# A trunk layer with three gated branches: every engine and the DMA queue run in the planner's order

## The chip, the cores and the metric

The kernel runs on one core of a Trainium2 chip. A core has a matrix engine (TensorE, PE in the profile), three engines for elementwise work (VectorE or DVE, ScalarE or ACT, GpSimd or POOL) and SyncE (SP), whose queue here issues every DMA. The engines run side by side, each through its own list of instructions from first to last, and wait for one another by semaphores. The metric is the device time of one execution in microseconds (us), taken as the median of several runs.

## The reference, cut to what is computed

One layer over 2048 tokens of width 1024. Every product with a weight is done in fp32 accuracy.

```python
h = rms_norm(x, norm_g)
z = h @ w_in
(aq, ak, av, af, az, bq, bk, bv, ba, bb, bz, mq, mz, gates) = _split_cols(z, IN_SIZES)
o_a = forgetting_attention(aq, ak, av, af + b_fg)      # 8 heads of 64
y_a = o_a * silu(az)
qkv = silu(causal_dwconv(concat([bq, bk, bv]), conv_w))
o_b = gated_delta_rule(gq, gk, gv, g_log, beta)        # 4 heads of 128
y_b = rms_norm(o_b, gdn_norm_g) * silu(bz)
mk, mv = split(rms_norm(mem, mem_norm_g) @ w_mem_kv)   # 256 memory rows
y_m = softmax(mq @ mk.T * scale) @ mv * silu(mz)
proj = einsum('bsnc,ncd->bsnd', stack([y_a, y_b, y_m]), w_branch)
merged = sum(sigmoid(gates + b_merge) * proj, axis=2)
return rms_norm(x + merged @ w_out, final_norm_g)
```

## The kernel before

The work is laid out over tokens in four groups of 512 and over features in blocks of 128. Each operand is split into a rounded part and a remainder (`hh` and `hl` for the activations, `wh` and `wl` for the weights), and `mm3k` multiplies them in three matmuls (L401, L402, L403). These "dense" jobs, made by `dense()`, are the bulk of PE's work; one weight block of 128 columns serves up to four groups (96 matmuls). Its path: a load `wr_in` by SP, a cast to `wh_in` on ACT (L381), the remainder `wl_in` on POOL (L385). Each result leaves PSUM through ACT and DVE (`evh` and `evl` for split results, `evt`, `evs`, `evg` for the others) and is stored to DRAM by SP (`dqh`, `dql`, `dgt` and so on).

The rest is written as generators that come one after another in `part_side`: norm (`part_norm`, which calls `rms_transposed`), logits (`part_logits`), memory attention, the chunks of the delta rule (`part_gdn_a`), their inverses (`part_gdn_inv`), the recurrence (`part_gdn_b` with `chain` and `tail`) and forgetting attention (`part_fox`). The last stages, branch projections (`pbr`, `pba`) and output projection (`pout`), belong to the dense part.

In the norm a tile of 128 tokens is loaded (`xt`), squared and summed on ACT (L342) or DVE (L335, `jkv`), its scale worked out on DVE (L347 and L293 to L298), multiplied in place (L352, `xt`), transposed on PE in two halves (L360, `ptx`), cast on ACT to `hh` (L362) and subtracted on DVE to `hl` (L363). Group 0 goes tile by tile, the other three in batches of four tiles.

In the logits, `pslg` on PE is followed by a chain of ACT and DVE steps that ends in a scan on DVE (L572, `loc`), a transpose on PE (`ptlg`) and a store `dG`. The inverse is a long row of small DVE steps (L901, L903) in the tiles `bk` and `tmp`, stored as `dinv`; the values `pd_v` leave through `evx` to the stores `dv` meanwhile. Forgetting attention clears its tiles `QA` and `KA` on DVE (L1115 to L1120), takes maxima of the scores `psm` (L1185, L1188), transposes them (`ptm`) and then makes the scores `pst` again for the exponent.

What sets the order: the class `Plan` (L25) holds a model of the time. Each generator yields the time from which its next PE step can run and what that step costs; `run` takes the first part that is ready at the modelled PE time, dense work being last in the list, and so emits the program. The costs are estimates (`act`, `dve`, `pool`, `dma`: an operation of n columns on DVE counts 0.15 + 0.00105 n us, a DMA 0.45 us of SP and at least 3 us to land), and `Ring` and `Banks` keep the modelled times at which PSUM comes free. `load_w`, `Feed` and `Stores` place weight loads and stores at modelled times in the same way. After that the framework has a scheduler of its own, which lays out each engine's list anew: by data dependences and its own estimates it may move an instruction past another of the same engine, DMAs on SP's queue included. The planner's order is thus only a suggestion to it.

Of the kernel before, what the change touches and what calls it, by code (L numbers as in the profile page):

```python
# [19 lines left out]
P = 128  # L20
EPS = 1e-6
INF = float("inf")
# [184 lines left out]
def four(ps):  # L207
    return ps.rearrange("p (a b) -> p a b", a=4)
# [3 lines left out]
def tile_trunk(ctx, tc, x, mem, norm_g, w_in, w_v, w_lg, b_fg, b_mg, conv_w, a_log, dt_b,  # L212
               gdn_g, mem_g, w_kv, w_br, w_out, final_g, out):
    nc = tc.nc
# [7 lines left out]
    pl = Plan()  # L222
# [20 lines left out]
    def move(dst, src, kb=0.0, after=0.0):  # L243
        nc.sync.dma_start(dst, src)  # L244
        return pl.dma(kb, after)
# [19 lines left out]
    dzb = [dram.tile([P, 4, 512], F32, name=f"dzb{g}") for g in range(NG)]  # L265
# [649 lines left out]
    def part_gdn_b():  # L915
# [7 lines left out]
        st = {"S": St0, "lev": 0, "chain": 0, "out": 0}  # L923

        def tmp(nm, tag, n):
            return gb.tile([P, 4, P], F32, tag=tag, name=nm, bufs=n)
# [63 lines left out]
        def chain():  # L990
            yield pl.pe + 2.0, 0.0
            for c in range(NCH):
                g, cc = divmod(c, 4)
# [4 lines left out]
                move(KV, dkv[c], 512)  # L998
                Aq = tmp("Aq", "Aq", 1)
                td = move(Aq, dau[c][:, :, 1, :], 256)  # L1000
                zb = tmp("zb", "zb", 1)
                move(zb, dzb[g][:, :, cc * P:(cc + 1) * P], 256)
                St = st["S"]
                yield later(td, lambda: inv[c][1] - 1.5 if c in inv else INF, rc.when), 0.88
                E, te = inv[c]
                pZ, kb = rc.take("pZ")
# [11 lines left out]
                pY, kb = rc.take("pY")  # L1018
# [8 lines left out]
                pS, kb = rc.take("pS")  # L1027
# [8 lines left out]
                pO, kb = rg.take("pO")  # L1036
                pO = four(pO)
# [2 lines left out]
                    nc.tensor.matmul(pO[:, h], Aq[:, h], Y[:, h], start=False, stop=True)  # L1040
                st["S"] = Sn
                st["chain"] = c + 1
                pl.add(tail(c, pO, kb, zb))

        def tail(c, pO, kb, zb):
            g, cc = divmod(c, 4)
            so = gb.tile([P, 4], F32, tag="so", name="so")
            jk = gb.tile([P, P], F32, tag="jk2", name="jk2")
            for h in range(4):
# [12 lines left out]
            pR, kb = rc.take("pR")  # L1062
# [15 lines left out]
            st["out"] = c + 1  # L1078

        pl.add(chain())  # L1080
        pl.add(levels())
        yield (lambda: 0.0 if st["out"] == NCH else INF), 0.0
# [668 lines left out]
    pl.run(dense())  # L1751


def _layout(i):
    import numpy as np
    c = np.ascontiguousarray
# [45 lines left out]
```

## Time and profile before

| | us |
|---|---|
| runs, median of 3 | 2633.79 (2629.45 to 2636.64) |
| profiled execution, own time | 2629.7 |
| its span | 2627.6 |
| PE busy | 2545.9 |
| DVE busy | 1338.9 |
| ACT busy | 1105.2 |
| POOL busy | 1013.1 |
| mean granted TensorE clock | 0.99 |

The stages in the span, by what PE runs: norm and first projections to 83 us, logits to 165, memory attention among dense jobs to 590, the delta rule's chunks among dense jobs to 1008, values to 1097, gates and recurrence to 1540, forgetting attention among gates to 2024, attention among branch projections to 2330, and the last branch with the output projection to the end. Times in the profile are us from the start of the span. In a row of the timeline stand the start, the duration, the engine, line and operation, and in square brackets how long the engine was idle before it and what ended that. In a row of windows stand the length, then for PE, PEld, DVE, ACT and POOL the busy time (and count of instructions), then the granted clock, the share of the DMA engines and GB/s. The records of matmuls overlap: one of 128 x 512 is 0.39 us long, while the next starts 0.23 us after it.

### The profile page before, as it was taken

The numbers are of one execution on the slowest core, as the hardware profiler recorded it, in microseconds if no ns is written. First come the engines' busy times: TensorE is split into PE (matmuls) and PEld (weight loads), VectorE is DVE, ScalarE is ACT, GpSimd is POOL, SyncE is SP. The second block draws the span as 40 slices with busy tenths as digits, with TensorE's granted clock in tenths as the row PEclk, the third lists the DMA queues.
The fourth block names the chain that finished last, engine by engine and source line by source line (L and its number), as shares of the span: only waits on it lengthen the run. The fifth ranks groups of instructions, "written<-read, shape, count | busy, mean of one in ns | idle before, by whom it ended". The sixth has DMA issues, their size and how long they took to land. (4 is left out here: it accounts for less than half of the span.)

```text
span 2627.6 us, 36711 instructions
## 1 busy us (share of the span) xinstructions
PE 2545.9 (97%) x12648; PEld 2112.2 (80%) x12648; DVE 1338.9 (51%) x2753; ACT 1105.2 (42%) x2287; POOL 1013.1 (39%) x818
## 2 busy tenths in 40 slices
PE   7998999999999999899999999999999999989998
PEld 6787888788888888688888888888887787877887
DVE  7452565656533337702222266666666677635433
ACT  5432234443475532134444446565556445323211
POOL 0101111221144334222232247777776768752110
PEclk9999999999999999999999999999999999999999
DMA  6223222222465564445555454344334768786432
GB/s 205 70 81 109 85 85 92 91 91 86 128 229 201 203 212 149 124 154 166 163 162 171 150 164 134 108 121 120 111 100 117 243 207 251 244 293 213 135 120 75
DMA packets 306050, 391.52 MB, mean 149 GB/s; under 512 B 62524, under 2 KB 185532, under 8 KB 305864
## 3 DMA queue, kind: packets, MB, share of 16 engines
q1 hardware_dynamic: 305864, 389.18, 46.5%
q8 instruction: 100, 1.64, 0.3%
q14 instruction: 86, 0.70, 0.1%
HBM read 238.78 MB, written 150.29 MB: 148 GB/s over the span
## 5 line engine op out<-in xcount | busy, mean ns | idle before, releaser
L401 PE MATMUL pd_in<-hh,wh_in 128*128 128x512 f32 x1856 | 746.6, 402 | 15.2 <-ACT evx L418 12.0
L403 PE MATMUL pd_in<-hh,wl_in 128*128 128x512 f32 x1856 | 728.2, 392 | 0.9
L402 PE MATMUL pd_in<-hl,wh_in 128*128 128x512 f32 x1856 | 726.0, 391 | 0.0
L385 POOL TENSOR_TENSOR wl_in<-wr_in,wh_in 128x1024 fp32r<-128x1024 f32 x84 | 202.5, 2411 | 626.0 <-ACT wh_in L381 597.8
L401 PEld LDWEIGHTS pd_in<-hh,wh_in 128*128 128x128 f32 x1856 | 350.1, 189 | 83.2 <-ACT evx L418 12.4
L403 PEld LDWEIGHTS pd_in<-hh,wl_in 128*128 128x128 f32 x1856 | 348.9, 188 | 78.6 <-POOL wl_in L385 4.0
L402 PEld LDWEIGHTS pd_in<-hl,wh_in 128*128 128x128 f32 x1856 | 350.3, 189 | 64.7
L1301 POOL TENSOR_TENSOR acc<-acc,ph 128x512 f32<-128x512 f32 (+3 forms) x288 | 318.9, 1107 | 55.7 <-ACT ph L1321 41.3
L1321 ACT ACTIVATE ph<-pst 128x512 fp32r<-128x512 f32 (+1 forms) x320 | 170.8, 534 | 159.7 <-PE pst L1315 81.2
L1278 DVE TENSOR_TENSOR plo<-pst,ph 128x512 fp32r<-128x512 f32 (+1 forms) x320 | 192.1, 607 | 83.3 <-ACT pst L1323 80.3
L1323 ACT ACTIVATE pst<-pst 128x512 f32<-128x512 f32 (+1 forms) x320 | 170.6, 533 | 0.0
L1573 POOL TENSOR_TENSOR gt<-gt,pp 128x512 f32<-128x512 f32 x64 | 86.7, 1358 | 191.6 <-DVE gt L1569 157.5
L381 ACT CAST wh_in<-wr_in 128x1024 fp32r<-128x1024 f32 x84 | 88.1, 1049 | 133.7 <-PE pd_in L402 119.2
L1188 DVE TENSOR_REDUCE nmx<-psm 128x1 f32<-128x512 f32 x192 | 128.5, 686 | 26.6 <-PE psm L1181 25.4
L1340 PE MATMUL po<-ph,Vs 128*128 128x512 f32 (+1 forms) x320 | 117.6, 368 | 1.1 <-ACT ph L1321 1.0
L474 DVE SCALAR_TENSOR_TENSOR evv<-xb,cw,evv 128x512 f32<-128x512 f32 x144 | 116.6, 810 | 3.7
L1314 PE MATMUL pst<-QA,KA 128*128 128x512 f32 (+1 forms) x320 | 116.2, 363 | 0.6 <-DVE QA L1196 0.6
L1315 PE MATMUL pst<-QB,KB 128*128 128x512 f32 (+1 forms) x320 | 116.6, 366 | 0.0
L1341 PE MATMUL pq<-plo,Vs 128*128 128x512 f32 (+1 forms) x320 | 116.1, 366 | 0.0
L1181 PE MATMUL psm<-KA,QA 68*128 68x512 f32 (+2 forms) x320 | 110.1, 375 | 4.6 <-DVE nmx L1188 3.0
L1541 PE MATMUL pbr<-yh,wbh 128*128 128x512 f32 x256 | 103.2, 404 | 9.3 <-DVE gt L1569 6.1
L1731 PE MATMUL pout<-woh,mh 128*128 128x512 f32 x256 | 100.1, 393 | 5.5 <-ACT woh L1643 5.5
(343 smaller groups left out, 4752.6 us busy)
## 6 DMA issues: line engine op xcount, KB each, us to landing
wr_in<-in_w_in SPq DMA_DIRECT2D x84, 512.0 KB
dgt<-evg SPq DMA_DIRECT2D x96, 256.0 KB
gt<-dgt SPq DMA_DIRECT2D x96, 256.0 KB
dpt<-gt SPq DMA_DIRECT2D x64, 256.0 KB
pp<-dpt SPq DMA_DIRECT2D x64, 256.0 KB
dgq<-evv SPq DMA_DIRECT2D x48, 256.0 KB
kqv<-dgq SPq DMA_DIRECT2D x16, 768.0 KB
xt<-in_x SPq DMA_DIRECT2D x16, 512.0 KB
```

Source lines behind the costliest of these rows:

```text
L385: nc.gpsimd.tensor_sub(lo, raw, hi.bitcast(F32))
L401: nc.tensor.matmul(ps, wh[:, k, :], xh[:, k, :], start=(k == 0), stop=False)
L402: nc.tensor.matmul(ps, wh[:, k, :], xl[:, k, :], start=False, stop=False)
L403: nc.tensor.matmul(ps, wl[:, k, :], xh[:, k, :], start=False, stop=(k == kt - 1))
L474: nc.vector.scalar_tensor_tensor(t, xb[:, j:j + 512], cw[:, wi, j:j + 1], t, ALU.mult, ALU.add)
L1188: nc.vector.tensor_reduce(mx, ps[:, 0:w], AX.X, ALU.max)
L1278: nc.vector.tensor_sub(plo[:, 0:w], ps[:, 0:w], ph[:, 0:w].bitcast(F32))
L1301: nc.gpsimd.tensor_add(acc[:, c0:512], acc[:, c0:512], ph[:, 0:w].bitcast(F32))
L1315: nc.tensor.matmul(ps[:, 0:w], KB[kt][:, ks], QBn[:, c0:512], start=False, stop=True)
L1321: nc.scalar.activation(ph[:, 0:w], ps[:, 0:w], AF.Exp, scale=0.125)
L1323: nc.scalar.activation(ps[:, 0:w], ps[:, 0:w], AF.Exp, scale=0.125)
L1340: nc.tensor.matmul(po[:, c0:512], V[:, 0:128], ph[:, 0:w], start=(t0 == 0), stop=(t0 == NT - 1))
```

## The change

At the end of the program every instruction of an engine is tied to the one emitted before it on the same engine, by an edge that orders the two for the scheduler and makes no wait on the chip. All five engines, SP with its DMAs among them, thereby get their lists in the order in which `Plan.run` emitted the program; instructions whose class name has "Pool" in it are left out of the chain. Further, the load of `zb` in the recurrence moves from `chain` to `tail`, where it is emitted once the previous chunk's output is out. What is computed stays the same. Line numbers above 1002 shift a little (L1315 before is L1316 now), those ahead of it not at all.

```diff
--- before.py
+++ after.py
@@ -998,8 +998,6 @@
                 move(KV, dkv[c], 512)
                 Aq = tmp("Aq", "Aq", 1)
                 td = move(Aq, dau[c][:, :, 1, :], 256)
-                zb = tmp("zb", "zb", 1)
-                move(zb, dzb[g][:, :, cc * P:(cc + 1) * P], 256)
                 St = st["S"]
                 yield later(td, lambda: inv[c][1] - 1.5 if c in inv else INF, rc.when), 0.88
                 E, te = inv[c]
@@ -1040,10 +1038,13 @@
                     nc.tensor.matmul(pO[:, h], Aq[:, h], Y[:, h], start=False, stop=True)
                 st["S"] = Sn
                 st["chain"] = c + 1
-                pl.add(tail(c, pO, kb, zb))
-
-        def tail(c, pO, kb, zb):
+                pl.add(tail(c, pO, kb))
+
+        def tail(c, pO, kb):
             g, cc = divmod(c, 4)
+            yield (lambda: 0.0 if st["out"] == c else INF), 0.0
+            zb = tmp("zb", "zb", 1)
+            move(zb, dzb[g][:, :, cc * P:(cc + 1) * P], 256)
             so = gb.tile([P, 4], F32, tag="so", name="so")
             jk = gb.tile([P, P], F32, tag="jk2", name="jk2")
             for h in range(4):
@@ -1751,6 +1752,15 @@
     pl.run(dense())
 
 
+    last = {}
+    for i in list(nc.cur_bb.bb.instructions):
+        if isinstance(i, mybir.Instruction) and "Pool" not in type(i).__name__:
+            if i.engine in last:
+                tc.add_manual_dep(i, last[i.engine].name, mybir.DependencyInfo(
+                    mybir.DependencyClass.NoSync, mybir.DependencyReason.DATA), reason="order")
+            last[i.engine] = i
+
+
 def _layout(i):
     import numpy as np
     c = np.ascontiguousarray
```

What this does to the lists is shown at three places. The first is DVE at the start of the program, in the norm of the first two tiles (`bmg` is the bias of the merge gates, scaled by a half once it is loaded). Before:

```order
L465 MEMSET xb 128x3
L347 TENSOR_SCALAR ss<-ss 128x1
L293 RECIPROCAL p0r<-p0s 128x1
L335 SCALAR_TENSOR_TENSOR jkv,ss<-xt 128x1024
L295 TENSOR_TENSOR p0t<-p0r 128x1
L347 TENSOR_SCALAR ss<-ss 128x1
L296 TENSOR_TENSOR p0t<-p0t,ss 128x1
L297 TENSOR_SCALAR p0t<-p0t 128x1
L293 RECIPROCAL p0r<-p0s 128x1
L298 TENSOR_TENSOR rs<-p0r,p0t 128x1
L295 TENSOR_TENSOR p0t<-p0r 128x1
L352 SCALAR_TENSOR_TENSOR xt<-xt,rs,g_bc 128x1024
```

After:

```order
L250 TENSOR_SCALAR bmg<-bmg 128x24
L347 TENSOR_SCALAR ss<-ss 128x1
L293 RECIPROCAL p0r<-p0s 128x1
L295 TENSOR_TENSOR p0t<-p0r 128x1
L296 TENSOR_TENSOR p0t<-p0t,ss 128x1
L297 TENSOR_SCALAR p0t<-p0t 128x1
L298 TENSOR_TENSOR rs<-p0r,p0t 128x1
L352 SCALAR_TENSOR_TENSOR xt<-xt,rs,g_bc 128x1024
L363 TENSOR_TENSOR hl_273<-ptx,hh_269 128x4x128 x2
L335 SCALAR_TENSOR_TENSOR jkv,ss<-xt 128x1024
L347 TENSOR_SCALAR ss<-ss 128x1
L293 RECIPROCAL p0r<-p0s 128x1
```

The scaling of `bmg` stood in row 22 before, behind four `hl` subtractions, and is now ahead of all the norm. The square of tile 1 (`jkv`) was early, now it follows tile 0's two `hl`. In the three later groups of the norm the lists differ in the same manner: four `xt` and then eight `hl` before, `xt` and two `hl` four times now.

The second is SP's queue around the logits (`lgraw`, `lgb` and `lgc` are their weights and constants, `dG` is the store of their scan, `wr_in` the weight of a dense job, `dqh` and `dql` stores of the first projection). Before:

```order
L244 DMA lgraw<-in_w_lg 128x128
L244 DMA lgb<-in_b_fg 8x1
L244 DMA lgb<-in_dt_b 4x1
L244 DMA lgc<-in_a_log 4x1
L244 DMA wr_in_0_1284<-in_w_in 128x1024
L244 DMA dqh_82<-evh 128x512
L244 DMA dql_86<-evl 128x512
L244 DMA wr_in_0_1455<-in_w_in 128x1024
L244 DMA dqh_82<-evh 128x512
L244 DMA dql_86<-evl 128x512
L244 DMA dzm_107<-evt 128x512
L244 DMA dG_140<-loc 4x512
```

After:

```order
L244 DMA lgraw<-in_w_lg 128x128
L244 DMA lgb<-in_b_fg 8x1
L244 DMA lgb<-in_dt_b 4x1
L244 DMA lgc<-in_a_log 4x1
L244 DMA dqh_82<-evh 128x512
L244 DMA dql_86<-evl 128x512
L244 DMA dG_140<-loc 4x512
L244 DMA wr_in_0_1052<-in_w_in 128x1024
L244 DMA dqh_82<-evh 128x512
L244 DMA dql_86<-evl 128x512
L244 DMA dG_141<-loc 4x512
L244 DMA wr_in_0_1113<-in_w_in 128x1024
```

The weights `wr_in_0_1052` and `wr_in_0_1113` stood in rows 10 and 12 before, among the loads of `xt`; now each is behind a store of `dG`.

The third is SP's queue at the end of the values (`dv` are their stores, `dinv` those of the inverse, `dgt` those of the gates). Before:

```order
L244 DMA dv_95<-evx 128x4x128 x8
L244 DMA dinv_194<-bk 128x1024
L244 DMA dinv_194<-tmp 128x1024
L244 DMA bk<-dblk_193 128x1024
L244 DMA dv_96<-evx 128x4x128 x8
L244 DMA dv_97<-evx 128x4x128 x6
L244 DMA dinv_195<-bk 128x1024
L244 DMA dinv_195<-tmp 128x1024
L244 DMA dv_97<-evx 128x4x128 x2
L244 DMA dv_98<-evx 128x4x128 x6
L244 DMA U<-dau_160 128x4x128
```

After:

```order
L244 DMA dv_97<-evx 128x4x128 x8
L244 DMA dv_98<-evx 128x4x128 x6
L244 DMA wr_in_0_9066<-in_w_in 128x1024
L244 DMA dv_98<-evx 128x4x128 x2
L244 DMA dgt_115<-evg 128x512
L244 DMA wr_in_0_9135<-in_w_in 128x1024
L244 DMA dgt_116<-evg 128x512
L244 DMA dgt_115<-evg 128x512
L244 DMA wr_in_0_9204<-in_w_in 128x1024
L244 DMA dgt_116<-evg 128x512
L244 DMA dinv_195<-bk 128x1024
L244 DMA dinv_195<-tmp 128x1024
```

`dinv_195` stood between the stores of `dv_97`; now it is behind all of `dv_98`, four gate stores and three weight loads. At the start of forgetting attention PE's list moves too: before, 27 dense matmuls stood between the fourth `psm` and the first `pst`, and now `ptm`, two `psm` and then `pst` follow it with no dense matmul between. In the last stage 192 `pba` matmuls stand in one block ahead of the first `pout`, where six `pout` came after the first 72 before.

## The prediction

> **What bounds the kernel now.** I read the page's busy shares first, then the windows of 66 us, then PE's waits.
>
> ```profile
> PE 2545.9 (97%) x12648; PEld 2112.2 (80%) x12648; DVE 1338.9 (51%) x2753; ACT 1105.2 (42%) x2287; POOL 1013.1 (39%) x818
> ...
> 0.00:66.00 66.00, 49.50 (x281) 41.36 (x282) 47.55 (x94) 35.87 (x68) 6.45 (x11) 0.97 0.60 204
> 66.00:132.00 66.00, 61.19 (x282) 47.58 (x281) 31.36 (x58) 32.89 (x43) 7.17 (x3) 0.97 0.21 69
> ...
> 1056.00:1122.00 66.00, 53.97 (x224) 43.23 (x223) 44.83 (x63) 14.46 (x33) 20.54 (x26) 0.90 0.45 129
> 1520.00:1586.00 66.00, 65.99 (x301) 53.20 (x300) 43.76 (x108) 28.61 (x55) 31.66 (x35) 1.00 0.50 154
> 1980.00:2046.00 66.00, 60.65 (x259) 47.20 (x258) 41.31 (x91) 36.69 (x77) 46.64 (x42) 0.95 0.52 154
> 2310.00:2376.00 66.00, 54.67 (x310) 47.57 (x308) 24.75 (x29) 16.80 (x24) 38.88 (x27) 0.92 0.79 270
> 2376.00:2442.00 66.00, 62.24 (x354) 54.63 (x353) 31.87 (x66) 18.04 (x37) 13.93 (x9) 0.97 0.56 186
> ```
>
> PE (TensorE) is the bound: busy 2545.9 of 2627.6 us, so only 81.7 us of the span are idle on it. In a stage like 1520 to 1586 it is full (65.99 of 66). It is not full in six windows: the head (16.5 us missing, then 4.8), 1056 to 1122 (12.0), 1980 to 2046 (5.4) and 2310 to 2442 (11.3 and 3.8). The matmuls stay the same, so the change can act in one way only: by making PE wait less there, or more somewhere. PE's waits say for what:
>
> ```profile
> PE pd_in L401 <- ACT evx L418: 12.0, 1, 12.0
> PE ptx L360 <- DVE p0t L296: 9.3, 1, 9.3
> ...
> PE pbr L1541 <- DVE gt L1569: 6.1, 2, 5.0
> PE pout L1731 <- ACT woh L1643: 5.5, 2, 3.1
> ...
> PE ptlg L579 <- DVE loc L572: 3.8, 1, 3.8
> ```
>
> PE's own order hardly moves (after the head it differs by some tens of matmuls). What moves is the order on DVE, ACT, POOL and in SP's queue that feeds PE. So I go through the places where a row that PE waits for stands behind another row than before.
>
> **The first tiles.** The scaling of `bmg` (L250) is now DVE's second row, ahead of the norm of tile 0.
>
> ```profile
> 4.71 0.50 SPq L244 DMA_DIRECT2D bmg<-in_b_mg  x1
> ...
> 5.34 0.15 DVE L347 TENSOR_SCALAR ss<-ss 128x1 f32<-128x1 f32 x1 [4.37 <-ACT jk L342]
> 5.84 1.21 DVE L335 SCALAR_TENSOR_TENSOR jkv<-xt 128x1024 f32<-128x1024 f32 x1
> ...
> 15.93 1.15 DVE L250 TENSOR_SCALAR bmg<-bmg 128x24 f32<-128x24 f32 x1
> ...
> 15.46 0.39 PE L402 MATMUL pdf<-hl,wh_in 128*128 128x256 f32 x1 [1.83 <-DVE hl L363]
> ...
> 25.55 0.38 PE L402 MATMUL pdf<-hl,wh_in 128*128 128x256 f32 x1 [0.22 <-DVE hl L363]
> ...
> DMA packets 974, 3.60 MB, mean 307 GB/s; under 512 B 96, under 2 KB 96, under 8 KB 974
> ...
> DMA packets 491, 0.23 MB, mean 334 GB/s; under 512 B 443, under 2 KB 443, under 8 KB 491
> ```
>
> `bmg` comes in rows of 96 bytes. The last two lines are the DMA views of 0 to 11.7 us (96 such small packets) and of 11.7 to 12.4 (443): behind 3.6 MB the small loads land at about 12.3. Before, L250 stood at 15.93 and held nobody; now tile 0's L347 starts at about 13 in place of 5.34. From there I count: norm chain 1.2, `xt` 1.3, to the first `hl` 2.6, second `hl` 0.6, so tile 0 is done near 18.7. Tile 1's square (1.21 us, L335), done before in the shadow at 5.84, now follows: 1.2 + 1.7 + 1.3 + 2.3 gives 25.5, where the first L402 stood at 15.46. Tiles 2 and 3 follow one after another, some 6.5 us each, so the second half starts near 39 in place of 25.55. **+14 us.** Bounds: +8, if half of the chain overlaps, to +18.
>
> **The other three groups of the norm.** DVE ran all four `xt` (partly beside the previous matmuls), then eight `hl`. Now it runs `xt`, two `hl`, `xt`, two `hl`.
>
> ```profile
> 45.15 3.68 DVE L352 SCALAR_TENSOR_TENSOR xt<-xt,rs,g_bc 128x1024 f32<-128x1024 f32 x3
> ...
> 52.40 1.88 DVE L363 TENSOR_TENSOR hl<-ptx,hh 128x512 fp32r<-128x512 f32 x3
> ...
> 50.97 1.47 PE L360 MATMUL ptx<-ident,xt 128*128 128x128 f32 x12
> 53.13 1.85 PE L360 MATMUL ptx<-ident,xt 128*128 128x128 f32 x12 [0.69 <-DVE hl L363]
> 55.19 1.25 PE L360 MATMUL ptx<-ident,xt 128*128 128x128 f32 x8 [0.21 <-DVE hl L363]
> ...
> 51.65 1.57 ACT L362 CAST hh<-ptx 128x512 fp32r<-128x512 f32 x3
> ```
>
> Before, a group's transposes took 50.97 to 56.5, 5.5 us between dense blocks. Now each tile is a closed circle: `xt` 1.23 (3.68 / 3), to the first half's `hh` 0.1 + 0.68, `hh` to `hl` 0.65 (51.65 + 0.59 is the first end, `hl` follows), two `hl` 1.29: 3.96 us. Group 1 has all four circles behind the last `evl`, 17.6 against 8.3: +9.3. In groups 2 and 3 the first `xt` still stands ahead of the last `evl`: 13.9 against 5.5, +8.4 each. **+26 us.** Bounds +12, if a circle cost only DVE's own 2.5 us, to +30. The memory rows at 196 go through the same helper, two tiles: **+2.**
>
> **The first logits.** The load of `wr_in_0_1052`, issued early before, now stands in SP's queue behind the store of `dG_140`, which waits for the scan L572.
>
> ```profile
> 86.77 0.40 PE L549 MATMUL pslg<-hh,wlh 128*128 128x512 f32 x1
> ...
> 100.49 1.22 DVE L572 TENSOR_TENSOR_SCAN loc<-rmask,l 64x512 f32<-64x512 f32 x1
> ...
> 1008.13 0.33 SPq L244 DMA_DIRECT2D wr_in<-in_w_in  x1
> ...
> 1011.75 1.05 ACT L381 CAST wh_in<-wr_in 128x1024 fp32r<-128x1024 f32 x1 [2.36 <-DMA wr_in<-in_w_in]
> ...
> L385 POOL TENSOR_TENSOR wl_in<-wr_in,wh_in x5: 2383/2390/3046, 10.1 to 115.8; 128x1024 fp32r<-128x1024 f32 x5
> ```
>
> From the end of the logits' matmuls (87.2) to the end of the scan (101.7) are 14.5 us; I take 12.5, since the weight's cast and an eviction leave the chain. Then 0.6 of issue, 4 to 5 us of landing (3.6 at 1008), cast 1.05, POOL 2.4. PE has some 6 us of work in these 21. **+16 us** (bounds +8 to +18). In exchange the wait of 3.8 us for `loc` at 117.5 goes, with its slow spell: **-6.**
>
> **Slow clock.** A stall of 2.6 us is followed by half clock:
>
> ```profile
> 2328.00:2331.00 3.00, 0.36 (x2) 0.00 (x0) 0.00 (x0) 0.00 (x0) 1.16 (x1) 1.00 0.77 225
> 2331.00:2338.00 7.00, 4.64 (x11) 3.69 (x12) 2.92 (x4) 1.85 (x3) 3.39 (x3) 0.52 0.84 292
> ...
> 1106.00:1119.00 13.00, 3.82 (x9) 3.05 (x10) 0.21 (x1) 4.72 (x11) 6.37 (x9) 0.50 0.91 265
> ```
>
> The granted clock is 0.52 for the 7 us after it, with 4.64 us of work: some 2.3 us lost. The longer head has about four sparse stretches more, each ended by dense work at half clock, at 1.7: **+7** (0 to 9). The Trainium skill, page "TensorE: Matmul & The Clock Gate", section "HAM oscillation — how this bites in real kernels", puts the limit at idle gaps over about 3.4 us. By that rule gaps of under 3 us inside the circles would cost no clock and this term would be near 0, the time 7 us lower. The row at 2328, a wait under 3 us, disagrees, so the row stands.
>
> **Values and inverse.** The 12.0 us wait for L418 at 1103: SP's store of `dinv_195`, behind DVE's inverse until 1105, blocks the value stores queued behind it; the buffers fill. Now that store stands behind all value stores and four gate stores. The 12.0 go, and half of the 3.82 us run at clock 0.50: **-14** (0 if another store blocks). The pieces of the value weight are cast later on ACT, behind two evictions: **+2.**
>
> **The recurrence.** `zb`'s load moves behind the previous output; it has the chunk's other matmuls and the dense gates as cover. **0**; without cover a load of about 4 us in each of 16 chunks, which I bound at -3 to +8 since PE stays full with gates there.
>
> **Start of forgetting attention.**
>
> ```profile
> 1534.25 1.02 DVE L1115 MEMSET QA<- 64x512 f32 x2 [5.69 <-DMA dyb<-zb]
> ...
> 1549.75 0.27 DVE L1185 CUSTOM_DVE_ANT_0 psm<-psm,mneg 128x128 f32<-128x128 f32 x1
> ```
>
> DVE clears tiles for 15.5 us ahead of the first maximum. Before, PE ran 27 dense matmuls of 0.23 us between the first score tile and `pst`; now `ptm`, two `psm` and six `pst` come directly, so those 6 to 7 us are waited out, then half clock: **+9** (+2 to +11).
>
> **Start of the branches and the end.** The first `pbr` now has 16 fewer attention matmuls ahead of it (16 x 0.23): **+4** (0 to 6). In 2310 to 2442 some 15 us are missing and some 6 go to slow clock. `gt` (L1569) no longer stands behind `yl`, and 192 `pba` matmuls run as one block, which gives `woh`, `wol` and `wbl` 20 us more. I let two thirds go: **-13** (-20 to 0).
>
> **Sum**: 14 + 26 + 2 + 16 - 6 + 7 - 14 + 2 + 0 + 9 + 4 - 13 = **+47**. On the profiled execution's 2629.7 that is 2676.7, call it **2677** (the median of the runs, 2633.8, lies 4.1 higher, inside my rounding).
>
> **Rivals.**
> *Faster: the circle overlaps.* If a tile's circle costs DVE's busy time alone (1.23 + 1.29 = 2.5 us), because PE's transposes and ACT's casts run beside it, as the `hh` and `hl` rows at 51.65 and 52.40 do, the groups lose 12 in place of 26, and the slow spells go (7). The head is then +14 + 12 + 2 + 16 - 6 = +38. If the fox and branch starts (13) also stay hidden and the values and the end return their full 14 + 20, the sum is +38 + 2 - 34 = +6. It turns negative from a circle of about 2 us or when `bmg` lands by 6 us, for then L250 costs nothing: -8 to -12, about 2619. Against it: within one tile `ptx` needs `xt`, `hl` needs `ptx`, and DVE takes no other row. Chance 0.18 for faster.
> *Same*: gains and losses cancel, or the edges are without effect. The rows differ on every engine but hardly on PE: 2632, chance 0.08.
> *Slower still: one late row holds a whole engine.* In 1540 to 2280 the `rl` rows and their `dR` stores wait behind other work in 64 row blocks; at 0.5 us each +32: 2709. PE's full 65.99 at 1520 speaks for slack. Chance 0.08.
> *Forecast*, 2645 to 2702: 0.66.
>
> **How the numbers follow.** 2622 to 2706 leaves out about 0.14 below (most of the faster case) and 0.06 above. A difference within 0.3% (7.9 us) can't be told from none. Faster 0.18, same 0.08, slower 0.74.
>
> **What would show it.** First dense L402 near 25.5, L250 ending at about 13; groups of `ptx` 14 to 18 us long; a PE wait for L381's cast or the `dG` store near 130 to 150; no wait for L418 after the values; a new wait of `ptm` or `psm` for L1185 at the fox start; fewer waits for L1569 and L1643 at the end. I am wrong if `ptx` groups stay near 6 us, or if waits appear in the stages I count as full.

## The result, and the profile after

| | before | after |
|---|---|---|
| runs, median | 2634.38 (2629.45 to 2636.64, 4 runs) | 2765.91 (2761.51 to 2767.45, 4 runs) |
| profiled execution, own time | 2629.7 | 2765.0 |
| its span | 2627.6 | 2763.3 |

All times are in us. The ratio of the runs is 1.0499, with a 95% interval of 1.048 to 1.0519. The change makes the kernel 5% slower. The forecast had the sign and a third of the size: +47 on the profiled execution, where it is +135.3, and 2766 lies far outside 2622 to 2706.

The page of the changed kernel, first the busy shares and then its slices (40 equal parts of the span, busy share in tenths, and in the last line the granted TensorE clock):

```profile
PE 2591.7 (94%) x12648; PEld 2148.6 (78%) x12648; DVE 1310.4 (47%) x2753; ACT 1105.3 (40%) x2285; POOL 1007.9 (36%) x818
...
PE   4787888999999999999999998999999999989998
...
PEclk8799899999999999999999999999999999999999
```

The same 12648 matmuls are busy for 45.8 us longer (2591.7 less 2545.9), since more of them run at a lower clock. PE's idle time rises from 81.7 to 171.6 (2763.3 less 2591.7), so by 89.9. The two make the span's 135.7. The digits under 9 fill the first seven slices, some 480 us. The windows of the changed kernel, at the same times as those of the kernel before (the work in them comes some 60 to 140 us later; in the columns: length, PE, PEld, DVE, ACT and POOL busy, granted clock, DMA share, GB/s):

```profile
0.00:66.00 66.00, 25.96 (x152) 23.22 (x152) 29.13 (x60) 20.05 (x37) 7.54 (x11) 0.89 0.37 136
66.00:132.00 66.00, 48.84 (x200) 39.13 (x201) 29.38 (x54) 24.18 (x45) 0.00 (x0) 0.75 0.18 65
...
264.00:330.00 66.00, 50.44 (x207) 41.15 (x206) 12.03 (x22) 13.20 (x22) 4.70 (x2) 0.78 0.24 77
330.00:396.00 66.00, 59.04 (x258) 48.19 (x258) 18.80 (x33) 13.48 (x21) 7.10 (x3) 0.90 0.25 80
...
1188.00:1254.00 66.00, 66.00 (x286) 53.38 (x285) 51.46 (x68) 13.70 (x33) 20.14 (x23) 1.00 0.43 132
1650.00:1716.00 66.00, 57.83 (x256) 47.05 (x255) 38.48 (x92) 24.59 (x44) 28.66 (x32) 0.92 0.55 156
2442.00:2508.00 66.00, 54.99 (x304) 48.11 (x302) 25.12 (x32) 18.85 (x27) 37.89 (x27) 0.90 0.91 317
...
287.00:290.00 3.00, 0.84 (x3) 0.30 (x2) 0.42 (x1) 1.32 (x2) 1.46 (x1) 0.98 0.00 0
290.00:296.50 6.50, 5.55 (x13) 4.45 (x14) 0.00 (x0) 0.00 (x0) 0.89 (x1) 0.50 0.00 0
```

and three rows of the kernel before that the prediction did not show, two windows and a row of PE's timeline:

```profile
198.00:264.00 66.00, 59.19 (x289) 49.86 (x290) 13.36 (x24) 14.66 (x24) 8.92 (x4) 0.95 0.33 109
264.00:330.00 66.00, 65.75 (x313) 54.64 (x312) 37.27 (x58) 18.84 (x29) 7.61 (x3) 1.00 0.26 79
...
204.55 1.97 PE L360 MATMUL ptx<-ident,xt 128*128 128x128 f32 x8 [8.16 <-DVE xt L352]
```

In the kernel before, PE was full between 264 and 330 (65.75 of 66 with 313 matmuls). From 198 to 264, where the memory rows stand, it was not: 6.8 us are missing there, and PE waits 8.16 for `xt`. In the changed kernel the window from 264 holds 207 matmuls, most of it work that the kernel before did between 190 and 240. A busy time of 50.44 understates the loss, because the clock is 0.78. The values' stage, 12.0 us short before, is full now (66.00 at 1188). The two rows at the bottom come back below.

PE's waits in the changed kernel (total, times, longest):

```profile
PE ptx L360 <- DVE xt L352: 66.1, 14, 16.3
PE pd_in L403 <- POOL wl_in L385: 12.7, 8, 1.7
PE pd_in L401 <- DVE evt L444: 11.7, 4, 7.9
PE ptlg L579 <- DVE loc L572: 10.2, 1, 10.2
PE pd_in L401 <- ACT wh_in L381: 8.9, 8, 2.6
PE ptm L1196 <- DVE mt L1192: 7.0, 1, 7.0
PE ptkv L654 <- ACT vt L644: 6.8, 4, 1.7
PE pba L1688 <- ACT wbh L1495: 5.2, 1, 5.2
...
PE pba L1690 <- POOL wbl L1497: 3.3, 3, 2.2
PE pout L1732 <- ACT woh L1644: 2.9, 1, 2.9
...
PE pbr L1542 <- DVE gt L1570: 1.5, 2, 1.3
```

The wait for `evx` (12.0) is gone. Three new groups stand out: `xt` with 66.1, then eight waits each for L385 and L381 (the casts and remainders of dense weights), and `evt` and `vt` of the memory stage. The eightfold ones are the forecast's blind spot.

**Where the 136 us come from.** The table follows fixed points of PE's work in both traces. Most are the k-th start of L401 (the hi matmul of the dense weights, `pdf`, `pd_in` and `pd_kv` together). Each number is the start in the changed kernel less that before; the third column is what the stretch since the row above adds.

| point of PE's work | shift | added | forecast |
|---|---|---|---|
| 65th L401 (last group of the norm) | +50.0 | +50 | 14 + 26 + 7 = +47 |
| 81st | +69.1 | +19 | +16 |
| 141st (logits done) | +62.4 | -7 | -6 |
| 261st (memory rows normed) | +88.4 | +26 | +2 |
| 561st (memory keys and values done) | +135.5 | +47 | none |
| 1221st (last before the values) | +135.9 | 0 | none |
| first `pd_v` | +142.5 | +7 | +2 |
| first `pZ` (recurrence starts) | +129.7 | -13 | -14 |
| first `psm` (recurrence ends) | +130.4 | +1 | 0 |
| 1701st (forgetting attention started) | +139.2 | +9 | +9 |
| first `pbr` (branches) | +129.3 | -10 | +4 |
| last `pout` | +135.7 | +6 | -13 |

Eight rows agree within 5 us. The last two that do not, the branches and the end, nearly cancel. The other two are one stretch: from the 141st to the 561st L401 the kernel before takes 297.1 us and the changed one 370.3. That is 73 us where the forecast has 2. The rows below show what happens there. ACT in the changed kernel (start, duration, line, operation, and in brackets the idle time before and what ended it):

```profile
259.26 0.63 ACT L342 ACTIVATE jk<-xt 128x512 f32<-128x512 f32 x1 [12.37 <-DMA xt<-in_mem]
...
287.15 0.37 ACT L611 CAST mkh<-pd_kv 128x256 fp32r<-128x256 f32 x1 [4.84 <-PE pd_kv L403]
287.42 1.05 ACT L381 CAST wh_in<-wr_in 128x1024 fp32r<-128x1024 f32 x1
...
2476.69 0.63 ACT L1659 ACTIVATE mh<-gt 128x512 fp32r<-128x512 f32 x1 [2.75 <-POOL gt L1574]
2477.23 0.60 ACT L1495 CAST wbh<-wbr 128x512 fp32r<-128x512 f32 x1
```

ACT before, at the same key job:

```profile
257.01 1.05 ACT L381 CAST wh_in<-wr_in 128x1024 fp32r<-128x1024 f32 x1 [4.67 <-PE pd_in L402]
...
260.91 0.37 ACT L611 CAST mkh<-pd_kv 128x256 fp32r<-128x256 f32 x1
```

PE in the changed kernel:

```profile
84.90 1.77 PE L360 MATMUL ptx<-ident,xt 128*128 128x128 f32 x8 [3.01 <-DVE xt L352]
89.36 1.94 PE L360 MATMUL ptx<-ident,xt 128*128 128x128 f32 x8 [2.68 <-DVE xt L352]
...
261.99 0.79 PE L401 MATMUL pd_in<-hh,wh_in 128*128 128x512 f32 x1 [7.94 <-DVE evt L444]
...
288.52 0.50 PE L401 MATMUL pd_in<-hh,wh_in 128*128 128x512 f32 x1 [1.41 <-ACT wh_in L381]
...
290.94 0.80 PE L403 MATMUL pd_in<-hh,wl_in 128*128 128x512 f32 x1 [1.70 <-POOL wl_in L385]
```

**Key and value jobs.** A short job over the 256 memory rows (`pd_kv`) stands between two wide dense jobs. Before, the next wide job's weight was cast at 257.01, 3.9 us ahead of the eviction `mkh`, under the last matmuls of the wide job. Now the cast stands directly behind `mkh`, which must wait for the end of the short job, and ACT sits idle for 4.84 us in front of it. So PE finishes the short job, waits 1.41 for the cast, runs two matmuls, waits 1.70 for POOL's remainder, and then runs at a clock of 0.50 until 296.5. The eight such jobs repeat this; the four value jobs wait less for the cast (0.51) and first 1.70 for `vt`.

**Memory rows.** ACT's square of the memory tile waits for its load (12.37 idle). DVE in the changed kernel shows who else stands behind it:

```profile
13.43 0.18 DVE L250 TENSOR_SCALAR bmg<-bmg 128x24 f32<-128x24 f32 x1 [12.50 <-DMA bmg<-in_b_mg]
...
260.77 0.15 DVE L344 TENSOR_REDUCE ss<-sp 128x1 f32<-128x2 f32 x1 [9.18 <-ACT jk L342]
...
261.25 1.29 DVE L444 SCALAR_TENSOR_TENSOR evt<-evt,pd_in 128x512 f32<-128x512 f32 x2
...
1683.39 0.16 DVE L1192 TENSOR_REDUCE mt<-nmx 128x4 fp32r<-128x4 f32 x1
```

DVE sits idle for 9.18 us in front of a reduction of 128 x 2, and two evictions `evt` of dense work, which empty PSUM, stand behind it. PE waits 7.94 us for one of them. A load that lands late thus holds ACT, DVE and PE, although the rows behind the waiting ones don't need it. Before, PE waited once in the memory rows (8.16), now twice (7.94 and 9.22).

### The profile page after: what moved, and what is told of

It is laid out like the page before. It is cut to its first block, busy times and chain, and to the rows that moved or that the text cites. A ratio compares the mean times of both kernels' runs of the same rounds, so it can differ in the third digit from the quotient of the medians.

```text
span 2763.3 us, 36434 instructions
## 1 busy us (share of the span) xinstructions
PE 2591.7 (94%) x12648; PEld 2148.6 (78%) x12648; DVE 1310.4 (47%) x2753; ACT 1105.3 (40%) x2285; POOL 1007.9 (36%) x818
## 5 line engine op out<-in xcount | busy, mean ns | idle before, releaser
L401 PE MATMUL pd_in<-hh,wh_in 128*128 128x512 f32 x1856 | 755.6, 407 | 25.7 <-DVE evt L444 11.7
L403 PE MATMUL pd_in<-hh,wl_in 128*128 128x512 f32 x1856 | 736.8, 397 | 12.7 <-POOL wl_in L385 12.7
L402 PE MATMUL pd_in<-hl,wh_in 128*128 128x512 f32 x1856 | 733.2, 395 | 0.0
L385 POOL TENSOR_TENSOR wl_in<-wr_in,wh_in 128x1024 fp32r<-128x1024 f32 x84 | 202.3, 2408 | 905.0 <-ACT wh_in L381 888.0
L401 PEld LDWEIGHTS pd_in<-hh,wh_in 128*128 128x128 f32 x1856 | 355.5, 192 | 98.3 <-DVE evt L444 13.4
L402 PEld LDWEIGHTS pd_in<-hl,wh_in 128*128 128x128 f32 x1856 | 355.2, 191 | 67.0
L1302 POOL TENSOR_TENSOR acc<-acc,ph 128x512 f32<-128x512 f32 (+3 forms) x288 | 319.2, 1108 | 34.5 <-ACT ph L1322 18.6
L1189 DVE TENSOR_REDUCE nmx<-psm 128x1 f32<-128x512 f32 x192 | 128.9, 687 | 62.1 <-PE psm L1182 61.2
L453 ACT ACTIVATE evg<-pd_in,bmg 128x512 f32<-128x512 f32 x96 | 66.1, 688 | 137.5 <-PE pd_in L403 121.8
L1315 PE MATMUL pst<-QA,KA 128*128 128x512 f32 (+1 forms) x320 | 117.2, 366 | 2.2 <-DVE plo L1279 2.2
L1316 PE MATMUL pst<-QB,KB 128*128 128x512 f32 (+1 forms) x320 | 117.1, 367 | 0.0
L474 DVE SCALAR_TENSOR_TENSOR evv<-xb,cw,evv 128x512 f32<-128x512 f32 x144 | 109.2, 758 | 5.1
```

The source lines that it names most:

```text
L385: nc.gpsimd.tensor_sub(lo, raw, hi.bitcast(F32))
L401: nc.tensor.matmul(ps, wh[:, k, :], xh[:, k, :], start=(k == 0), stop=False)
L402: nc.tensor.matmul(ps, wh[:, k, :], xl[:, k, :], start=False, stop=False)
L403: nc.tensor.matmul(ps, wl[:, k, :], xh[:, k, :], start=False, stop=(k == kt - 1))
L1189: nc.vector.tensor_reduce(mx, ps[:, 0:w], AX.X, ALU.max)
L1302: nc.gpsimd.tensor_add(acc[:, c0:512], acc[:, c0:512], ph[:, 0:w].bitcast(F32))
```

## The experiments

My theory A after the result: the loss comes from rows that could run, standing behind a row that waits, on ACT, DVE or SP, and each place has its own engine. Rivals: PE's own order makes the loss (called B in the text for PE, C further down), or the loads on the DMA queue come late (B in the texts for ACT and SP). "Before" in brackets is the kernel before, run on the same chip. Each time is of one run, except for the last three versions.

**One engine at a time.** The edges stay on one engine alone; the others are free. The edit, with `Activation`, `DVE` and `SP` in the place of `PE` for the other three:

```diff
-        if isinstance(i, mybir.Instruction) and "Pool" not in type(i).__name__:
+        if isinstance(i, mybir.Instruction) and "Pool" not in type(i).__name__ and i.engine == mybir.EngineType.PE:
```

PE: 

> Edges on TensorE alone (zb's load moved as in the change). The new trace puts the loss of 131 us at four places: +50 us to the 65th matmul of L401 (norm), +13 in the logits, +63 from the 141st to the 561st matmul of L401 (297 us before, 370 after: memory rows and weights of the memory keys), +10 at the start of forgetting attention. Theory A: the order on the engines that feed TensorE makes all of these but the last. Then this kernel is within 15 us of before (2625 to 2650), with the third stretch at 295 to 302 us and perhaps +5 to +10 at the start of forgetting attention. Theory B: TensorE's own order makes the loss; then the total is above 2700 and the third stretch above 330 us.

ACT: 

> Edges on ScalarE alone. Theory A: the stretch from the 141st to the 561st matmul of L401 is long because the cast of the next weight (L381) stands behind the eviction of the short memory-key job, eight times about 3 us of waiting and 3 us of half clock; then this stretch takes 335 to 355 us (297 before, 370 after) in this kernel, and the norm's first 65 matmuls end within 6 us of before's 73.4. Total 2665 to 2695. Theory B (the loads on the DMA queue come late): this stretch stays under 305 us here and the total under 2645.

DVE: 

> Edges on VectorE alone. Theory A: the norm is VectorE's: bmg's scaling ahead of the first tile and the order xt, two hl; the 65th matmul of L401 starts at 115 to 125 us (73.4 before, 123.4 after), and the stretch of the memory keys (141st to 561st) takes 295 to 312 us. Total 2670 to 2690, since the values' stall of before stays. Rival: the norm is slowed by the DMA queue or ScalarE as well; then the 65th matmul starts before 100 us.

SP: 

> Edges on the DMA queue alone. Theory A: the queue's order is worth +10 to +16 us in the logits (weight behind the store of dG), some +10 in the memory rows (loads behind the dF stores), and takes away the 12 us stall after the values and its half clock (-14); the stretch of the memory keys takes 300 to 312 us. Total 2630 to 2650. Theory B: the loads make the memory keys' loss: that stretch takes over 335 us and the total is over 2670.

| edges on | time (before 2636.91) | norm, to the 65th L401 | memory rows, 141st to 261st | keys and values, 261st to 501st | 501st to 561st |
|---|---|---|---|---|---|
| none (before) | | | 94.3 | 151.3 | 51.6 |
| PE | 2681.6 | +4.3 | 95.2 | 155.7 | 58.1 |
| ACT | 2697.4 | +17.0 | 103.9 | 183.4 | 51.7 |
| DVE | 2717.8 | +50.8 | 108.2 | 151.5 | 51.0 |
| SP | 2676.7 | +1.4 | 104.3 | 152.6 | 51.5 |
| all | | +50.0 | 120.3 | 188.7 | 61.2 |

The columns are read from the traces. The totals with PE, DVE and SP held lie 27 to 32 us above what was expected, that with ACT 2, and ACT costs 17 in the norm where 6 was the limit: with one engine held and the others laid out around it, each version loses in other places, so their totals are no parts of a sum. The stretches are clear, though. The norm's loss is there whole with DVE alone held. Of the keys' loss of 37, ACT alone makes 32 (183.4 for 151.3). The memory rows lose 10 to 14 with ACT, DVE or SP alone. From the 501st to the 561st only PE shows a loss. Both theories B fell for the whole stretch from the 141st to the 561st: it stayed under 312 us with PE, DVE or SP held (with PE 308.9, 7 us above theory A's range; B expected over 330 with PE and over 335 with SP), and went to 339.0 with ACT. Only the total with SP, 2676.7, is as B had it (over 2670).

**Only the weight casts free.** All edges, but the cast L381 stays out of ACT's chain.

```diff
...
-            nc.scalar.copy(hi, raw)
+            nc.scalar.copy(hi, raw); free.add(nc.cur_bb.bb.instructions[-1].name)
...
-        if isinstance(i, mybir.Instruction) and "Pool" not in type(i).__name__:
+        if isinstance(i, mybir.Instruction) and "Pool" not in type(i).__name__ and i.name not in free:
```

> All edges of the change, but the casts of the dense weights (L381, on ScalarE) are left out of the chain, so that the scheduler may place them ahead of the evictions. Theory A (the memory keys' loss is this cast behind the eviction L611 or L475, and the half clock that follows): the stretch from the 141st to the 561st matmul of L401 takes 315 to 335 us, against 370 with all edges and 297 before; the rest of the loss (memory rows, some 25 us) stays. Total 2710 to 2735 (2766 with all edges). Rival (the remainder on GpSimd or the load sets the pace): the stretch stays over 355 us and the total over 2750.

It took 2749.6 (2629.4), 16 us less than with all edges, and the stretch 342.8 in place of 370.3. Expected were 2710 to 2735 and 315 to 335, so both missed. PE's waits from 205 to 549 in this version:

```profile
PE ptkv L654 <- ACT vt L644: 16.6, 4, 4.2
PE pd_in L401 <- DVE evt L444: 9.9, 2, 8.6
PE ptx L360 <- DVE xt L352: 9.1, 1, 9.1
...
PE pd_in L403 <- POOL wl_in L385: 2.1, 2, 1.3
```

The waits for L381 are gone and those for L385 fall from 12.7 to 2.1, but `ptkv` now waits 16.6 for `vt`, where it waited 6.8. The casts were one part, and part of what they gave was taken back by the next row in the chain.

**Casts emitted earlier.** All edges; the planner emits a dense weight's cast 3 us ahead of its modelled landing.

```diff
...
-            self.pl.at(t, lambda: self.landed(use, tile))
+            self.pl.at(t - self.early, lambda: self.landed(use, tile))
...
-    w_feed = Feed(pl, 2)
+    w_feed = Feed(pl, 2, 3.0)
...
-            t = pl.act(kt * P, pl.pe)
+            t = pl.act(kt * P, pl.pe + 3.0)
```

> All edges, and one number of the planner changed: the cast of a dense weight is emitted 3 us ahead of the modelled landing of its load, which puts it ahead of the eviction of the short memory job (rows 95 and 96 of ScalarE) while the loads stay in place. Theory A: from the 261st to the 501st matmul of L401 (151 us before, 189 with all edges, 175 with the casts free) it takes 155 to 168 us, and the weight waits of L401 and L403 (21.6 us with all edges) fall under 8. Total 2728 to 2748. Rival (the cast then waits for its load and holds the evictions): over 180 us, total over 2755.

It took 2773.3 (2631.0) where 2728 to 2748 was expected, and the stretch from the 261st to the 501st L401 179.6, at the rival's end. For the first key job the mechanism is confirmed: the cast starts at 278.28, ahead of `mkh` at 282.86, and the next stretch (261st to 321st) takes 39.9, near the 38.6 before. The value jobs still lose (10.6 by waits for `vt`). By the 561st L401 it is 25 us ahead of the changed kernel; the later stages were planned anew, so its total says nothing on the casts.

**The memory stage by itself, and with one engine let go.** Edges only on what is emitted from dense job 3 to dense job 23 (the number of instructions at each job's start is kept in `mk`); then the same without ACT; then the same without SP.

```diff
...
-    for i in list(nc.cur_bb.bb.instructions):
-        if isinstance(i, mybir.Instruction) and "Pool" not in type(i).__name__:
+    for k, i in enumerate(list(nc.cur_bb.bb.instructions)):
+        if isinstance(i, mybir.Instruction) and "Pool" not in type(i).__name__ and mk[3] <= k < mk[24]:
...
+        ... and mk[3] <= k < mk[24] and i.engine != mybir.EngineType.Activation:
...
+        ... and mk[3] <= k < mk[24] and i.engine != mybir.EngineType.SP:
```

All engines: 

> Edges only on what is emitted from the fourth dense job up to the first one after the memory attention's queries (the memory rows, the eight memory-key and memory-value jobs and the memory attention), none elsewhere. Theory A: the loss of this part is made here and needs no edges elsewhere; the stretch from the 141st to the 561st matmul of L401 takes 350 to 372 us (297 before, 370 with all edges), everything else is as before, total 2685 to 2705. Rival (the loss is handed on from the late head): the stretch stays under 325 us, total under 2660.

Without ACT: 

> The edges stand over dense jobs 3 to 23 alone (memory rows, memory keys and values), on PE, DVE and SP; ACT's list stays free. With ACT in the chain the stretch from the 141st to the 561st L401 took 364.2 us, before 297.1. Theory A (the cast L381, held behind an eviction of the short memory job on ACT, makes most of the key and value jobs' loss): the stretch falls to 320 to 340, the row PE pd_in L401 <- ACT wh_in L381 falls under 4 us, total 2655 to 2685. Theory C (the order on PE itself, transposes directly behind pd_kv, makes it): the stretch stays above 355 and total above 2695. The memory rows' part (141st to 201st and 261st L401) stays as it was with ACT chained, 115 to 122 us, by both.

Without SP: 

> The same stretch of edges, on PE, DVE and ACT, with SP's queue free. Theory A (SP's order, the loads of the memory rows behind the stores dF, makes the loss ahead of the key jobs): from the 141st to the 261st L401 falls from about 116 us to 95 to 103, the key and value jobs (261st to 561st) stay within 10 us of the run with SP chained, total 2680 to 2700. Rival (the closed circle of xt and hl on DVE and the weight's path make it): it stays above 110.

| edges over jobs 3 to 23 | time (before) | 141st to 261st | 261st to 501st | 501st to 561st | whole stretch |
|---|---|---|---|---|---|
| none | | 94.3 | 151.3 | 51.6 | 297.1 |
| all engines | 2707.1 (2631.0) | 115.9 | 187.2 | 61.2 | 364.3 |
| all but ACT | 2667.9 (2634.5) | 106.9 | 153.8 | 60.6 | 321.2 |
| all but SP | 2703.2 (2634.5) | 117.6 | 185.7 | 58.7 | 361.9 |

Edges over this stretch alone reproduce 67 of its 73 us and 76 of the whole kernel's 132, and after the 681st L401 the shift stays at 73 to the recurrence. The loss is local; the total lies 2 us above its range. Without ACT's edges, ACT in the same place is:

```profile
274.26 1.05 ACT L381 CAST wh_in<-wr_in 128x1024 fp32r<-128x1024 f32 x1 [0.41 <-DMA wr_in<-in_w_in]
...
276.10 0.37 ACT L611 CAST mkh<-pd_kv 128x256 fp32r<-128x256 f32 x1 [0.79 <-PE pd_kv L403]
```

and PE's waits from 147 to 510 are:

```profile
PE pd_in L401 <- DVE evt L444: 7.4, 1, 7.4
PE ptx L360 <- DVE xt L352: 7.3, 1, 7.3
...
PE pd_in L403 <- POOL wl_in L385: 2.0, 2, 1.3
PE ptkv L654 <- ACT vt L644: 1.9, 4, 0.5
```

The cast is ahead of `mkh` again and waits only for its load. No wait for L381 is left among PE's waits, and the stretch from the 261st to the 501st L401 falls from 187.2 to 153.8, 2.5 above no edges at all. PE's order from the 261st to the 501st is the same in both (and with PE alone held, 155.7), so theory C fell for the keys and values: **they lose by ACT's order.** What was missed is the memory rows, expected at 115 to 122 by both theories: 106.9, so 9 of their 21.6 us are ACT's too. Letting SP go gains nothing while the others are held; the rival held there (117.6 in place of 95 to 103, and a total 3 us above the range), though SP held alone costs 10. With ACT free, the 7.4 for `evt` stays, and with DVE alone held the part from the 141st to the 201st takes 57.5 (46.2 before, 55.9 with all edges), where L344 stands idle 9.04 in front of `evt` and PE waits 6.4 for it (2.4 are a wait for `loc` of the logits, which came later there). So the first half of the memory rows is DVE's row in front of `evt`. What is left from the 501st to the 561st, 9 us, stays with ACT free, and 6.5 of it are there with PE alone held.

**The norm.** All edges; `bmg` is scaled after the first group, and a batch's four `xt` are emitted ahead of its eight `hl`.

```diff
-        nc.vector.tensor_scalar(bmg, bmg, 0.5, None, ALU.mult)
...
-                t2 = pl.dve(D, t1)
+                t2s.append(pl.dve(D, t1))
+            for t in range(t0, t0 + batch):
+                xt, t2 = xts[t - t0], t2s[t - t0]
...
-            hready[0] = hhalf[1]
+            hready[0] = hhalf[1]; nc.vector.tensor_scalar(bmg, bmg, 0.5, None, ALU.mult)
```

> All edges, with two pieces of the norm emitted in another order: bmg's scaling after the first group, and in the batches of four the four products xt ahead of the eight hl. Theory A: the first L402 of the projection starts at 17 to 19.5 us (25.5 was worked out and about 26.9 seen with all edges, 15.46 before), each of the three later groups loses 0 to 2 us against before in place of about 11, and the 65th matmul of L401 starts at 84 to 94 us (123.4 with all edges, 73.4 before). Total 2725 to 2740. Rival (the groups are held by ScalarE's or the queue's order, not VectorE's): the 65th matmul starts after 105 us.

It took 2726.5 (2629.4). The 65th L401 came at 92.0 in place of 123.4 (73.4 before), and the last two groups lose 1.2 us each where they lost 10.6 and 10.8. The closed circle made the groups' loss. Two expectations missed: the first L402 stands at 21.7 (17 to 19.5), and the first of the three groups still loses 5.6 (0 to 2; 11.6 with all edges). 18.6 us are left, 16.3 of them by the start of the second group's matmuls; the first group still goes tile by tile.

**The `zb` move alone.** No edges.

```diff
-    last = {}
-    for i in list(nc.cur_bb.bb.instructions):
...
-            last[i.engine] = i
```

> No edges at all, only zb's load moved into tail. Theory A: it is worth nothing, total 2625 to 2645. Rival (the load was needed early, or its new place shifts the scheduler's order elsewhere): over 2650 or under 2620.

2628.1 (2629.4): worth nothing, as forecast.

**Where the order helps.** Edges only from dense job 24 on; then without the first 30 planned us of forgetting attention and the last stage; then also without the dense jobs from 36 up to the values; at last without jobs 24 to 35 too. `mk` holds the instruction numbers at which these stages begin (`val` the values, `fox0` forgetting attention, `fox1` 30 us behind it, `last` the last stage). The four conditions in the loop:

```diff
+ k >= mk[24]
+ mk[24] <= k < mk['fox0'] or mk['fox1'] <= k < mk['last']
+ mk[24] <= k < mk[36] or mk['val'] <= k < mk['fox0'] or mk['fox1'] <= k < mk['last']
+ mk['val'] <= k < mk['fox0'] or mk['fox1'] <= k < mk['last']
```

> Edges only from the dense job after the memory attention's queries on (job 24 of the list), none in the norm, the logits and the memory part. Theory A: the loss lies in the part without edges here; from there to the end the change gains and loses the same (-1 us between the two traces), so the total is 2628 to 2645 and the 621st matmul of L401 starts within 8 us of before's 513.5. Rival (a late order is spoiled by an early one, or the early order by the late): the total is over 2660.

> Edges only where the two traces show no loss: from the first dense job after the memory attention's queries, without the first 30 planned us of forgetting attention and without the last stage. Theory A: -7 at the end of the values, nothing at the start of forgetting attention in place of +8, -6 at the start of the branches, -5 in them, 0 in the last stage: total 2608 to 2622, ratio 0.990 to 0.996. Rival (the free pieces between chained ones are placed badly): 2630 or more.

> As the other, and also without edges in the eight dense jobs ahead of the values, where the new trace waits 4.6 us for VectorE and runs 3.4 us at half clock. Theory A: another 5 to 7 us less: total 2602 to 2618. Rival (the stall after the values comes back): as much as the other or more.

> Edges only where the runs so far showed a gain or nothing: from the values to the start of forgetting attention, and from 30 planned us behind that start to the last stage. None on dense jobs ahead of the values, at the fox start or in the last stage. Theory A (the gains stand by themselves): 2608 to 2622, ratio 0.992 to 0.997, about the same as the version that also had edges from job 24 to 35. Rival (the gain of the middle is given back in the last stage whatever stands before it): over 2625.

| edges | time | before | ratio, 95% interval |
|---|---|---|---|
| from job 24 | 2630.9 | 2629.4 | one run |
| without the fox start and last stage | 2625.3 | 2631.0 | 0.9975 (0.9965 to 0.9984) |
| also without the jobs ahead of the values | 2621.3 | 2631.0 | 0.9961 (0.9948 to 0.9974) |
| values to fox, and fox to last stage | 2618.8 | 2634.5 | 0.9943 (0.993 to 0.9957) |

The last is 0.6% faster than the kernel before, little but clear of its interval. In its trace the values give back 13 us, at the first `pbr` the shift is -18.2, at the last `pbr` -21.1, and at the end -9.7. So 11 us are lost in the last stage, although no edge stands there. The version with edges in that stage loses 11 as well (-9.8 at the last `pbr`, +1.5 at the end). The gain of the middle holds, but half of it is given back, by something that is not the edges of that stage; the rival of the last text was half right, and the middle two versions each missed their range by 3 us for it. ACT in the last version, in that stage:

```profile
2330.57 0.63 ACT L1660 ACTIVATE mh<-gt 128x512 fp32r<-128x512 f32 x1 [1.90 <-POOL gt L1575]
2331.11 0.60 ACT L1496 CAST wbh<-wbr 128x512 fp32r<-128x512 f32 x1
```

The cast of `wbh` stands behind an `mh` that waits for `gt`, as in the changed kernel (the rows at 2476.69 and 2477.23), and PE waits 5.6 for it, which the kernel before does not do in this stage. With PE or SP alone held, the stage loses 9.5 and 13.5, and PE waits 4.3 and 5.7 for `wbh` there. So the wait comes without any edge on ACT; why it comes stays open.

## Why the forecast was a third of the size

**The step that failed** is the one that decided which places to cost: "PE's own order hardly moves ... So I go through the places where a row that PE waits for stands behind another row than before." The list that followed had no dense weight of the stage from 141 to 561, although L381 and L385 are rows that PE waits for, and the order of ACT there shows the cast moved from ahead of `mkh` to behind it. I had taken the slack of a wide dense job (96 matmuls 0.23 us apart) for all of them. The short job between two wide ones is about 5 us long (`pd_kv` from some 282 to 287), the cast cannot start until it ends, and cast and remainder take 1.05 and 2.35. So no slack is left. The windows I counted as full (65.75 of 66 from 264 on) told only that PE did not wait there before; they say nothing of how little would be needed. One more window than the six I named was not full, 198 to 264 with 59.19, and it holds the memory rows. The runs put 47 us on the keys and values, 32 to 33 of them on ACT's order (183.4 with ACT alone held, 187.2 to 153.8 with ACT let go), and the sign for being wrong that the prediction named, waits in the stages counted as full, is what came.

**The memory rows**, "the same helper, two tiles: +2", were 26. The term had priced the circle of `xt` and `hl`, as in the norm. It left out what stands behind the waiting rows: DVE's `evt` behind L344, and ACT's rows behind L342.

**The norm: right, by its steps.** L250 ended at 13.6 (forecast 13). The first dense matmul came 13.7 later and the first of the second half 17.0 (forecast 14), and the three groups cost 33 with the slow clock (26 + 7). A group has transposes 4.46 us apart at 84.90 and 89.36, where a circle of 3.96 was worked out: at half clock PE's eight transposes take 1.94 us, against 1.03 at 108.34 at full clock. The first L402 stands at 27.4 and not 25.5. (Three sums of the prediction come out lower than written: 25.2 for 25.5, 13.5 for 14, and 15 for the 16 of the logits; little hangs on it.)

**The first logits: right in number, in part in cause.** +19 and -7 for +16 and -6. The `wr_in` load goes out at 150.3, directly behind the `dG` store of 149.9, as forecast. But PE's wait shows at the transpose of `loc` (10.2), which no dense matmul covers, and not at the cast. With SP alone held, the stretch from the 65th to the 81st L401 loses 17.7, but with PE alone held 19.9: SP's order is enough for this loss, and PE's own order, which the forecast left out, is too.

**Slow clock: right in kind, too small**, as it was counted in the head alone. The trace shows 8 stretches of half clock before, 48 us together, and 21 after, 174 us (the last one, at the end of the span, left out); the difference is 126 us, worth at most 63 at half speed, and 45.8 by PE's busy time. Ten of the new ones lie in the stage that was left out. The Trainium skill, page "TensorE: Matmul & The Clock Gate", section "HAM oscillation — how this bites in real kernels", sets the limit at idle gaps over about 3.4 us. Here two waits of 1.41 and 1.70 with two matmuls between are followed by 6.5 us at 0.50 (the rows at 287 and 290); no single gap reaches 3.4, so a plan that looks only for the longest gap misses this loss. Which share of idle time brings half clock on was not measured. The row at 2328 that the prediction set against the rule was misread: the window of 3 us cuts a wait that is 5.0 us long, the one for `gt` in the prediction's own list, so that row agrees with the rule.

**Values -13 (forecast -14), recurrence +1 (0), start of forgetting attention +9 (+9): right.** With SP alone held PE's wait for `evx` is gone; with PE, ACT or DVE alone it stays (10.2, 2.3 and 15.3). The start's wait is `ptm` for `mt` (7.0), which stands at 1683.39 behind DVE's clearing of tiles, as forecast. The value weight's pieces, forecast at 2, cost PE a wait of 1.0. The 7 us ahead of the values are another row's: a dense matmul waits 4.6 for `evl`, in front of which DVE stood idle 13.40 for a store `dkh` (its row at 1142.44), with 3.4 us of half clock behind it.

**Branches and end: wrong in sign, small.** From the start of forgetting attention to the branches the kernel gains 10 where +4 was forecast. The versions with edges there gain too, but which rows make the gain wasn't tried. The end loses 6 where -13 was forecast. Up to the first `pba` it gains 4.8: the waits for `gt` fall from 6.1 to 1.5, as argued. From there on it loses 11.2. The step "192 `pba` matmuls run as one block, which gives `woh`, `wol` and `wbl` 20 us more" left `wbh` out: its cast at 2477.23 stands behind `mh`, which waits for POOL's `gt`, and PE waits 5.2 for it, 3.3 for `wbl` and 2.9 for `woh`. From the first `pba` to the last `pout` PE is idle 16.2 us where it was 10.1, and the half clock there is 20.5 us where it was 6.8. Since the version without edges in this stage loses as much, with the same wait for `wbh`, the block of 192 matmuls is not shown to be the cause.

**The rivals.** "One late row holds a whole engine" was the mechanism that decided, with a chance of 0.08 and in the wrong stage: I had looked for it at 1540 to 2280, where rows are long and slack is real, and not where jobs are short.

## What to carry to other kernels

When every engine is held to one written order, look first for short jobs between long ones: the weight of the next job must be cast ahead of the eviction of the short one, or its cast waits for the whole job. For each moved row that waits, list what stands behind it on its engine and who waits for that, in the full stages above all, for a full window shows no slack. An order kept for whole stretches (here the values and forgetting attention) can gain while the same rule loses elsewhere, so apply it by stage and check each stage's end.

## What was not expected of the hardware

Half clock came after waits as short as 1.41 and 1.70 us close together, and its stretches in the trace are 3.4, 6.8, 10.2, 13.7 or 17.1 us long. A row of 0.15 us on DVE (L344) could stop PE for 7.94 us, by way of an eviction behind it. Holding a single engine to the planner's order cost 40 to 81 us over before on its own (2676.7 to 2717.8 against 2636.9), while two of the four engines show under 5 us of it in the norm. My reading, which no run tests, is that the loss moves to where the free engines no longer fit the held one.
